# A recurrent branch on one core: four channel tiles projected with the tokens held still, and the stage put in another order

## The chip, the cores and the metric

The kernel runs on one core of a Trainium2 chip. The metric is device time in microseconds (us) of one execution; the kernel before takes 966.03 us (median of three runs, 965.65 to 968.62). A change of less than about 0.3%, 2.9 us, can't be told from none by such runs.

The engines are named as the profile names them: PE is the matrix engine (PEld its weight loads), DVE the vector engine, ACT the scalar engine, POOL the general-purpose one, SP the engine that issues nearly all transfers.

## What is computed

A two-layer decoder trunk over 256 tokens of 1024 channels, all in float32. Layer 0 is FFN, recurrent block, FFN; then keys and values are made; layer 1 is FFN, attention, FFN. The change touches the recurrent block alone:

```python
def recurrent_block(x, w_in, conv_w, conv_b, w_a, b_a, w_x, b_x, lam, w_out):
    gx = x @ w_in                                   # 1024 -> 2 * 1344
    gate, rec = gx[..., :D_RNN], gx[..., D_RNN:]
    rec = causal_depthwise_conv(rec, conv_w, conv_b)  # 4 taps along the tokens
    rec = rg_lru(rec, w_a, b_a, w_x, b_x, lam)        # block-diagonal gates, then a scan along the tokens
    return (jax.nn.gelu(gate) * rec) @ w_out
```

## The kernel before

**Tiles.** The 256 tokens are two token tiles, t = 0 and 1, of 128. The 1344 recurrent channels are eleven channel tiles: ten of 126 and one of 84. Channel tiles are worked in pairs p = 0 to 5 (the last pair is the one tile of 84), and pairs in batches of two: batch 0 is tiles 0 to 3, batch 1 tiles 4 to 7, batch 2 tiles 8 to 10.

**Split weights.** Every product is made of three matmuls, because each operand is split into an upper and a lower part: upper by upper, upper by lower, lower by upper. The normalized tokens are there as `xhi` and `xlo`. Each block of weights goes through a unit: a transfer on SP's queue into `raw` (`load_raw`, five buffers), then ACT writes the upper part `whi` (L173) and DVE subtracts to get the lower part `wlo` (L177); there are nine buffers of each. SP, ACT, DVE and POOL each work strictly in their own order; PE's order is written by hand.

**Two ways to project.** The gate half is projected by gate units (`add_gate_unit`): 128 tokens are held in PE and up to 512 columns of weights move past them (L183 to L185, form 128x512), eight blocks of 128 input channels deep, two per unit. The result lies with tokens on partitions. The recurrent half is projected by rec units (`add_rec_units`, named r0 to r5 after their pair): 126 columns of weights are held and the 256 tokens move (L190 to L192, form 128x256). The result lies with channels on partitions and tokens along the row, which the convolution and the scan need.

**After the projection.** `conv(p, ps)` scales and biases the tile with ACT (L748), then DVE adds three taps (L754). `gw0` to `gw5` are the block-diagonal gates of a pair on PE (L795), followed by tanh (L809), tanh and exp (L828) on ACT, and a chain on DVE. After each second pair a batch follows: square roots on ACT (L853) and GELU of the token tile 1 gates (L856), products and scans on DVE (L861, L862, L867), then y, the product with the gate, split by ACT (L887) and DVE (L892) for the output projection. Tanh and exp share a function table with neither the roots nor the GELU, so that ACT loads a table at each change.

**Turning.** Gate values of token tile 0 for batches 0 and 1 are brought to channels on partitions by `gate_turn`: POOL copies the 16-bit halves of the values apart into `pl` (L700), a transposing transfer on SP's queue (`swap`, L216) writes `turned`, and POOL joins the halves again (`join`, L220). The others are turned on PE (L877).

**Order of the stage.** `RG_ORDER` lists what PE does: `0g3` is gate unit 3 on token tile 0, `r2` both units of pair 2, `gw1` the gates of pair 1. The order of the entries also counts time: each slot ends in a tick, `defer(n, f)` runs f some ticks later, and a purse of ticks doles out the queued DVE work. `OUT_ORDER` then gives the output projection: token tile 0 with tiles 0 to 7, token tile 1 with tiles 0 to 5, token tile 0 with tiles 8 to 10, and the rest. The tile framework orders ACT, DVE, POOL and SP from this and puts in the waits.

Of the kernel before, what the change touches and what calls it, by code (L numbers as in the profile page):

```python
# [9 lines left out]
F32 = mybir.dt.float32  # L10
F32R = mybir.dt.float32r
BF16 = mybir.dt.bfloat16
U16 = mybir.dt.uint16
# [30 lines left out]
def trunk_kernel(ctx: ExitStack, tc: tile.TileContext, A: dict, out: bass.AP):  # L44
# [17 lines left out]
    def mmbank():  # L62
        return psum.tile([P, 512], F32, tag="mm", name=nm("mm"), bufs=4)
# [17 lines left out]
    def defer(n, fn):  # L81
        pend.append([n, fn])
# [60 lines left out]
    def main_x(t, k):  # L143
        return xhi[:, k, t * P:(t + 1) * P], xlo[:, k, t * P:(t + 1) * P]
# [22 lines left out]
    def split(rawv, parts, n, pieces=1, pin=False):  # L167
        u = Unit()
        hi = wpool.tile([P, 1024], F32R, tag="whi", name=nm("whi"), bufs=WB)
        lo = wpool.tile([P, 1024], F32R, tag="wlo", name=nm("wlo"), bufs=WB)  # L170
        m = n // pieces
        for c in range(0, n, m):
            up = nc.scalar.activation(hi[:parts, c:c + m], rawv[:, c:c + m], AF.Copy)  # L173
            if settled[0] or pin:
                tc.keep_in_program_order(up)
                settled[0] = False
            nc.vector.tensor_tensor(lo[:parts, c:c + m], rawv[:, c:c + m], hi[:parts, c:c + m].bitcast(F32), ALU.subtract)  # L177
        u.hi, u.lo = hi[:parts, :n], lo[:parts, :n]
        return u
# [38 lines left out]
    def join(dst, turned):  # L218

        nc.gpsimd.tensor_copy(dst, turned.rearrange("p (h f) -> p h f", h=2))  # L220
# [436 lines left out]
    def w_in(c0, n, k0, kn):  # L657
        return A["rg_w_in"][0, k0 * P:(k0 + kn) * P, c0:c0 + n].rearrange("(k p) n -> p k n", p=P)
# [6 lines left out]
    def add_gate_unit(g, k0, kn):  # L665
        c0, nn = GCOLS[g]

        def prep():
            return split(load_raw(w_in(c0, nn, k0, kn), P, kn * nn), P, kn * nn)

        def work(t, u):
            if k0 == 0:
                gacc[(g, t)] = mmbank()
            ps = gacc[(g, t)][:, :nn]
            for j in range(kn):
                k = k0 + j
                mm3(ps, *main_x(t, k), u.hi[:, j * nn:(j + 1) * nn], u.lo[:, j * nn:(j + 1) * nn], k == 0, k == 7)
            if k0 + kn == 8:

                if t not in toks:  # L680
                    toks[t] = pools["r"].tile([P, DRNN], F32, name=f"tok{t}")
                tok = toks[t][:, c0:c0 + nn]
                if t == 0 and g < 2:
                    nc.scalar.activation(tok, ps, AF.Gelu_apprx_tanh)
                    defer(5 - 3 * g, lambda: gate_turn(g))
                else:
                    nc.scalar.activation(tok, ps, AF.Copy)
                    plain.append(tok)
        rg[f"g{sum(n[0] == 'g' and n[1] != 'w' for n in rg)}"] = len(items)
        items.append((prep, work))  # L690
# [3 lines left out]
    def gate_turn(g):  # L694

        halves = hpool.tile([P, 512], F32, tag="t1", name=nm("pl"), bufs=2).bitcast(U16)
        hv = halves.rearrange("p (h j f) -> p h j f", h=2, j=4)
        src = toks[0][:, 4 * g * RT:4 * (g + 1) * RT].bitcast(U16)
        nc.gpsimd.memset(hv[:, :, :, RT:], 0)
        nc.gpsimd.tensor_copy(hv[:, :, :, :RT], src.rearrange("p (j f h) -> p h j f", h=2, f=RT))  # L700
# [4 lines left out]
        defer(4, lambda: join(flat, turned))  # L705

    def tiles_of(p):
        return [2 * p, 2 * p + 1] if p < 5 else [10]
# [4 lines left out]
    def add_rec_units(p):  # L713
        tl = tiles_of(p)
        n = sum(width(i) for i in tl)
        c0 = DRNN + tl[0] * RT
        ks = [(0, 4), (4, 4)] if p < 5 else [(0, 8)]
        got = []
        for (k0, kn) in ks:
            def prep(k0=k0, kn=kn):  # L720
                return split(load_raw(w_in(c0, n, k0, kn), P, kn * n), P, kn * n)

            def work(t, u, k0=k0, kn=kn):
                got.append(u)
# [12 lines left out]
                conv(p, ps)  # L737
            rg[f"r{p}{'ab'[k0 // 4]}"] = len(items)
            items.append((prep, work))

    def conv(p, ps):
        tl, w = tiles_of(p), pw(p)
        if p >= 4:
            flush(("y", (p - 4) // 2))
        xc = pools["r"].tile([RT, 2, S], F32, tag="xc", name=nm("xc"), bufs=4)
        xcs[p] = xc
        for j, i in enumerate(tl):
            nc.scalar.activation(xc[:w, j, :], ps[:w, j * S:(j + 1) * S], AF.Identity,  # L748
                                 bias=par[:w, 4 * NRT + i:4 * NRT + i + 1], scale=par[:w, 3 * NRT + i:3 * NRT + i + 1])

        def taps(j, i):
            for k in (2, 1, 0):
                s = 3 - k
                nc.vector.scalar_tensor_tensor(xc[:w, j, s:], ps[:w, j * S:(j + 1) * S - s],  # L754
                                               par[:w, k * NRT + i:k * NRT + i + 1], xc[:w, j, s:], ALU.mult, ALU.add)
# [151 lines left out]
    def parts_of(g):  # L907
        return [(0, 4, RT)] if g < 2 else [(0, 2, RT), (2, 3, BLK)]

    for g in range(2):  # L910
        for k0 in range(0, 8, 2):
            add_gate_unit(g, k0, 2)
    for p in range(4):
        add_rec_units(p)
    for k0 in (0, 3, 6):
        add_gate_unit(2, k0, min(3, 8 - k0))
    add_rec_units(4)
# [1 line left out]
    for p in range(6):  # L919
        gw_unit(p)  # L920
    n_rg = len(items)
    RG_ORDER = ("0g0 0g1 0g2 0g3 0g4 0g5 0g6 0g7 1g0 1g1 r0 1g2 r1 gw0 1g3 1g4 r2 gw1 1g5 1g6 r3 gw2 1g7 "
                "0g8 0g9 0g10 r4 gw3 r5 1g8 gw4 1g9 1g10 gw5").split()
    OUT_ORDER = [0] * 8 + [1] * 6 + [0] * 3 + [1] * 5

    gbox = {}
# [543 lines left out]
```

## Time and profile before

| | |
|---|---|
| median of three runs | 966.03 us |
| the profiled execution, its own time | 965.92 us |
| its span on the core, first to last instruction | 964.2 us |
| PE busy | 955.9 us, 99% of the span |
| DVE, ACT, POOL busy | 640.7, 527.6, 218.2 us |
| TensorE clock granted | 0.999 of full speed |

The recurrent stage lies between about 189.6 us, its first projection, and about 297 us, the end of its output projection, in the times of that span. The busy time of PE is the union of matmuls that overlap: each 128x512 matmul is shown as lasting 0.39 us, though the next starts 0.23 us after it, so the pace of PE is read from starts and not from durations.

### The profile page before, as it was taken

How to read it: one execution, taken by the hardware profiler on the slowest of the kernel's cores; microseconds unless marked ns; L12 is line 12 of the kernel's file. 1: busy time of each engine (PE TensorE's matmuls, PEld its weight loads, DVE VectorE, ACT ScalarE, POOL GpSimd, SP SyncE). 2: the span in 40 equal slices, each digit the busy share in tenths (PEclk: the TensorE clock that was granted, in tenths of full speed). 3: DMA queues.
4: the chain of work that ended last, by engine and by line, in shares of the span. 5: the costliest groups of instructions: out<-in, count | busy, mean ns of one | idle time of the engine just before them, and what ended most of it. 6: DMA issues, size and time to landing. Idle time of an engine off the chain costs nothing.

```text
span 964.2 us, 12866 instructions
## 1 busy us (share of the span) xinstructions
PE 955.9 (99%) x4575; PEld 791.3 (82%) x4575; DVE 640.7 (66%) x845; ACT 527.6 (55%) x750; POOL 218.2 (23%) x221
## 2 busy tenths in 40 slices
PE   9999999999999999999999999999999999999997
PEld 6888888898878888888898888888887788888886
DVE  6658674678997666664686566665488876666642
ACT  7546453568886555443565455444366855444431
POOL 2712330130001323230003522234022012232200
PEclk9999999999999999999999999999999999999999
DMA  8787995475346787775558979878773468777731
GB/s 286 226 258 225 256 284 197 142 228 163 119 123 219 209 236 211 205 242 196 135 182 278 253 219 258 230 216 265 226 256 97 133 199 236 207 222 233 223 109 44
DMA packets 148934, 198.79 MB, mean 206 GB/s; under 512 B 67166, under 2 KB 85958, under 8 KB 148742
## 3 DMA queue, kind: packets, MB, share of 16 engines
q1 hardware_dynamic: 146182, 191.06, 65.6%
q0 software_dynamic: 2080, 6.38, 2.1%
q8 instruction: 36, 0.59, 0.2%
q10 hardware_dynamic: 608, 0.53, 0.2%
q14 instruction: 28, 0.23, 0.1%
HBM read 182.19 MB, written 3.16 MB: 192 GB/s over the span
## 4 chain that ended last, share of the span: by engine, by line
PE 95%; DVE 2%; ACT 1%; issue 1%; POOL 0%; DMA 0%; POOLq 0%; DVEq 0%; ACTq 0%
PE mm L428 16%; PE mm L429 16%; PE mm L432 16%; PE mm L183 13%; PE mm L185 13%; PE mm L184 13%; PE gt L795 2%; PE mm L1305 1%; PE mm L190 1%; PE mm L191 1%; PE mm L192 1%; PE gt L226 1%; ACT pe L1181 1%; DVE wlo L177 0%; PE tr L127 0%
## 5 line engine op out<-in xcount | busy, mean ns | idle before, releaser
L177 DVE TENSOR_TENSOR wlo<-raw,whi 128x1024 fp32r<-128x1024 f32 (+5 forms) x329 | 418.0, 1276 | 230.7 <-ACT whi L173 228.3
L173 ACT ACTIVATE whi<-raw 128x1024 fp32r<-128x1024 f32 (+5 forms) x329 | 341.9, 1045 | 308.6 <-PE mm L432 119.2
L428 PE MATMUL mm<-whi,xhi 128*128 128x512 f32 x656 | 256.6, 391 | 0.0
L429 PE MATMUL mm<-wlo,xhi 128*128 128x512 f32 x656 | 255.5, 389 | 0.0
L432 PE MATMUL mm<-whi,xlo 128*128 128x512 f32 x656 | 202.1, 389 | 0.0
L428 PEld LDWEIGHTS mm<-whi,xhi 128*128 128x128 f32 x656 | 123.2, 188 | 25.9 <-issue 0.7
L432 PEld LDWEIGHTS mm<-whi,xlo 128*128 128x128 f32 x656 | 123.1, 188 | 25.8 <-DVE xlo L240 0.2
L429 PEld LDWEIGHTS mm<-wlo,xhi 128*128 128x128 f32 x656 | 123.2, 188 | 25.4 <-DVE wlo L177 0.3
L183 PE MATMUL mm<-whi,hhi 128*128 128x512 f32 x352 | 137.2, 390 | 0.0
L185 PE MATMUL mm<-whi,hlo 128*128 128x512 f32 x352 | 137.0, 389 | 0.0
L184 PE MATMUL mm<-wlo,hhi 128*128 128x512 f32 x352 | 136.9, 389 | 0.0
L540 POOL COPY pl<-prod 128x1024 uint16<-128x1024 uint16 (+1 forms) x48 | 69.9, 1456 | 174.4 <-DMA prod<-pl 174.4
L527 POOL COPY pl<-prod 128x1024 uint16<-128x1024 uint16 (+1 forms) x48 | 66.3, 1382 | 151.9 <-DVE prod L524 86.8
L183 PEld LDWEIGHTS mm<-whi,hhi 128*128 128x128 f32 x352 | 66.1, 188 | 13.7
L185 PEld LDWEIGHTS mm<-whi,hlo 128*128 128x128 f32 x352 | 66.1, 188 | 13.7
L184 PEld LDWEIGHTS mm<-wlo,hhi 128*128 128x128 f32 x352 | 66.1, 188 | 13.6
L198 POOL TENSOR_SCALAR nv<-ss 128x1 f32<-128x1 f32 x22 | 9.6, 437 | 268.7 <-ACT junk L205 268.7
L524 DVE SCALAR_TENSOR_TENSOR prod<-mm,rstd,sil 128x512 f32<-128x512 f32 (+1 forms) x48 | 33.8, 703 | 29.5 <-PE mm L432 25.9
L515 ACT ACTIVATE sil<-mm,rstd 128x512 f32<-128x512 f32 (+1 forms) x48 | 31.0, 649 | 32.9 <-PE mm L432 25.0
L546 DVE TENSOR_TENSOR hlo<-pl,hhi 128x512 fp32r<-128x512 f32 (+1 forms) x48 | 41.2, 858 | 3.7 <-ACT hhi L545 3.7
L183 PE MATMUL mm<-whi,xhi 128*128 128x512 f32 (+1 forms) x112 | 42.8, 382 | 0.0
L185 PE MATMUL mm<-whi,xlo 128*128 128x512 f32 (+1 forms) x112 | 42.5, 379 | 0.0
(223 smaller groups left out, 1054.6 us busy)
## 6 DMA issues: line engine op xcount, KB each, us to landing
raw<-in_ffn_w_down_dram SPq DMA_DIRECT2D x88, 512.0 KB
raw<-in_ffn_w_up_dram SPq DMA_DIRECT2D x80, 512.0 KB
raw<-in_ffn_w_gate_dram SPq DMA_DIRECT2D x78, 512.0 KB
raw<-in_rg_w_in_dram SPq DMA_DIRECT2D x10, 504.0 KB
raw<-in_rg_w_out_dram SPq DMA_DIRECT2D x10, 504.0 KB
raw<-in_ffn_w_gate_dram SPq DMA_DIRECT2D x19, 256.0 KB
raw<-in_ffn_w_up_dram SPq DMA_DIRECT2D x16, 256.0 KB
raw<-in_rg_w_in_dram SPq DMA_DIRECT2D x8, 512.0 KB
```

Of the source, the lines that this page charges most:

```text
L173: up = nc.scalar.activation(hi[:parts, c:c + m], rawv[:, c:c + m], AF.Copy)
L177: nc.vector.tensor_tensor(lo[:parts, c:c + m], rawv[:, c:c + m], hi[:parts, c:c + m].bitcast(F32), ALU.subtract)
L183: nc.tensor.matmul(ps, xh, wh, start=first, stop=False)
L184: nc.tensor.matmul(ps, xh, wl, start=False, stop=False)
L185: nc.tensor.matmul(ps, xl, wh, start=False, stop=last)
L428: nc.tensor.matmul(ps, get_x(t, k)[0], u.hi[:, c], start=k == 0, stop=False)
L429: nc.tensor.matmul(ps, get_x(t, k)[0], u.lo[:, c], start=False, stop=False)
L432: nc.tensor.matmul(ps, get_x(t, k)[1], u.hi[:, c], start=False, stop=k == nk - 1)
L524: nc.vector.scalar_tensor_tensor(pr[:, :nn], ps, rs[t][:, 0:1], s, ALU.mult, ALU.mult)
L527: nc.gpsimd.tensor_copy(halves.rearrange("p (h f) -> p h f", h=2), pr[:, :nn].bitcast(U16).rearrange("p (f h) -> p h f", h=2))
L540: nc.gpsimd.tensor_copy(halves.rearrange("p (f h) -> p h f", h=2), turned.rearrange("p (h a) b -> p h (a b)", h=2))
L546: keep(nc.vector.tensor_tensor(lv, x, hv.bitcast(F32), ALU.subtract))
```

## The change

The four channel tiles of pairs 0 and 1 are no longer projected by rec units. New units R0 to R3 (`add_tok_unit`) hold 128 tokens and move 504 columns of weights past them, as the gate units do: two blocks of input channels per unit, for both token tiles. The result `rtok` is copied from the accumulator by ACT (L725). POOL copies its halves apart into `pl` (L730), a transposing transfer turns it, and POOL writes it into its half of `rT` (L737), once for each token tile. The convolutions of pairs 0 and 1 then read `rT` in place of an accumulator, and start seven and eight ticks after the second token tile's last R unit.

The list of the stage is rewritten: R units first, the gate unit loads of group 1 behind pair 2's. `gate_turn` runs two ticks after its GELU for both groups.

```diff
-                    defer(5 - 3 * g, lambda: gate_turn(g))
+                    defer(2, lambda: gate_turn(g))
...
+    def add_tok_unit(k0, kn):
+        nn = 4 * RT
+        def prep():
+            return split(load_raw(w_in(DRNN, nn, k0, kn), P, kn * nn), P, kn * nn)
+        def work(t, u):
+            if k0 == 0:
+                racc[t] = mmbank()
+            ps = racc[t][:, :nn]
+            for j in range(kn):
+                k = k0 + j
+                mm3(ps, *main_x(t, k), u.hi[:, j * nn:(j + 1) * nn], u.lo[:, j * nn:(j + 1) * nn], k == 0, k == 7)
+            if k0 + kn == 8:
+                tok = pools["r"].tile([P, 4, P], F32, tag="y", name=nm("rtok"), bufs=2).rearrange("p a b -> p (a b)")
+                nc.scalar.activation(tok[:, :nn], ps, AF.Copy)
+                halves = pools["r"].tile([P, 2, S], F32, tag="xc", name=nm("pl"), bufs=4).rearrange("p a b -> p (a b)")
...
+                nc.gpsimd.memset(hv[:, :, :, RT:], 0)
+                nc.gpsimd.tensor_copy(hv[:, :, :, :RT],
+                                      tok[:, :nn].bitcast(U16).rearrange("p (j f h) -> p h j f", h=2, f=RT))
+                if t == 0:
+                    rtok["T"] = pools["r"].tile([P, 4, S], F32, tag="tt", name=nm("rT"), bufs=3)
+                turned = tok.bitcast(U16)
+                dst = rtok["T"][:, :, t * P:(t + 1) * P].bitcast(U16).rearrange("p a (b h) -> p h a b", h=2)
+                defer(1, lambda: swap(turned, halves))
+                defer(4, lambda: nc.gpsimd.tensor_copy(dst, turned.rearrange("p (h a b) -> p h a b", h=2, a=4)))
+                if t == 1:
+                    for p in range(2):
+                        defer(7 + p, lambda p=p: conv(p, rtok["T"][:, 2 * p:2 * p + 2, :].rearrange("p a b -> p (a b)")))
...
-    RG_ORDER = ("0g0 0g1 0g2 0g3 0g4 0g5 0g6 0g7 1g0 1g1 r0 1g2 r1 gw0 1g3 1g4 r2 gw1 1g5 1g6 r3 gw2 1g7 "
-                "0g8 0g9 0g10 r4 gw3 r5 1g8 gw4 1g9 1g10 gw5").split()
+    RG_ORDER = ("0R0 0R1 0R2 0R3 0g0 0g1 0g2 0g3 1R0 1R1 1R2 1R3 1g0 1g1 1g2 1g3 r2 0g4 0g5 0g6 0g7 gw0 1g4 gw1 "
+                "1g5 r3 gw2 1g6 1g7 0g8 0g9 0g10 r4 gw3 r5 1g8 gw4 1g9 1g10 gw5").split()
```

On POOL, at the start of the stage, the change has these rows after the statistics of the second token tile (`rtok_356` and `rtok_375` are the two token tiles of the new projection, `tok0` the gates of token tile 0):

```order
L730 COPY pl_357_1826<-rtok_356_1824 128x8x126
L699 MEMSET pl_366_1904 128x8x2
L699 MEMSET pl_408_2129 128x8x2
L737 COPY rT_358_1829<-rtok_356_1824 128x2x4x128
L700 COPY pl_366_1904<-tok0_1882 128x8x126
L220 COPY tokT_368_1908<-turned_367_1907 128x2x512
L730 COPY pl_376_1935<-rtok_375_1933 128x8x126
L737 COPY rT_358_1829<-rtok_375_1933 128x2x4x128
```

Before, only the two gate groups were turned here. Now the join of the gates' group 0 (L220) stands ahead of the copy that opens the turning of `rtok` for token tile 1 (the second L730).

On ACT, late in the stage, from the y of batch 1 to the last roots of batch 2 (`th_458`, `tt_469` belong to pairs 4 and 5, the names of 84x256 rows to pair 5), the rows before are:

```order
L887 ACTIVATE y_465_2588<-y_464_2587 126x512
L887 ACTIVATE y_465_2588<-y_467_2592 126x512
L828 ACTIVATE th_458_2533<-th_458_2533,sp4_102 126x256
L809 ACTIVATE th_470_2606<-gt_468_2597,hb_97 84x256
L809 ACTIVATE th_471_2607<-gt_468_2597,hb_97 84x256
L828 ACTIVATE tt_469_2600<-th_470_2606,sp2_101 84x256
L173 ACTIVATE whi_478_2645<-raw_477_2643 126x1024
L828 ACTIVATE th_470_2606<-th_470_2606,sp4_102 84x256
L173 ACTIVATE whi_481_2661<-raw_480_2659 126x1024
L853 ACT_TABLE_LOAD
L853 ACTIVATE tt_469_2600<-tt_469_2600 126x512
L853 ACTIVATE tt_469_2600<-tt_469_2600 84x256
```

and with the change, from the second y on:

```order
L927 ACTIVATE y_473_2561<-y_475_2565 126x512
L868 ACTIVATE tt_485_2589<-th_463_2500,sp2_101 126x256
L868 ACT_TABLE_LOAD
L868 ACTIVATE th_463_2500<-th_463_2500,sp4_102 126x256 x2
L173 ACTIVATE whi_489_2621<-raw_488_2619 126x1024
L868 ACTIVATE tt_485_2589<-th_480_2579,sp2_101 84x256
L893 ACT_TABLE_LOAD
L893 ACTIVATE tt_485_2589<-tt_485_2589 126x512
L868 ACT_TABLE_LOAD
L868 ACTIVATE th_480_2579<-th_480_2579,sp4_102 84x256
L173 ACTIVATE whi_494_2680<-raw_493_2678 126x1024
L893 ACT_TABLE_LOAD
```

The roots of pairs 4 and 5 are now apart, with the exp of pair 5 between them: two more table loads, and the exps of pair 4 stand behind the y of batch 1. The root of pair 5 follows on the last row.

On DVE, shortly before the first lower part of y for tiles 8 and 9 (`y_495` before, `y_503` with the change), the change has:

```order
L901 TENSOR_SCALAR tt_485_2589<-th_481_2580,tt_485_2589 84x256
L926 TENSOR_TENSOR y_507_2724<-tr_500_2701,tt_485_2589 126x256
L902 TENSOR_TENSOR tt_485_2589<-tt_485_2589,xc_456_2467 84x256
L177 TENSOR_TENSOR wlo_498_2694<-raw_496_2691,whi_497_2693 84x1024
L907 TENSOR_SCALAR tt_485_2589<-th_480_2579,tt_485_2589 84x256
L177 TENSOR_TENSOR wlo_506_2721<-raw_504_2718,whi_505_2720 128x1024
L926 TENSOR_TENSOR y_501_2705<-tr_499_2697,tt_485_2589 84x128
L926 TENSOR_TENSOR y_507_2724<-tr_500_2701,tt_485_2589 84x128
L932 TENSOR_TENSOR y_503_2707<-y_501_2705,y_502_2706 126x256
```

The last row, the lower part that the output projection needs for tile 8, stands behind the work of the last tile of 84 and two weight splits here as it did before; what those rows wait for is the root of pair 5. Outside the recurrent stage and the first rows of the FFN behind it the order of all engines is unchanged.

More of the change, by code (lines that the diff above doesn't have):

```diff
@@ L705, in gate_turn @@
         defer(4, lambda: join(flat, turned))
+    racc, rtok = {}, {}
+    def add_tok_unit(k0, kn):
[13 more added lines that the diff above has]
+                halves = pools["r"].tile([P, 2, S], F32, tag="xc", name=nm("pl"), bufs=4).rearrange("p a b -> p (a b)")
+                halves = halves.bitcast(U16)
+                hv = halves.rearrange("p (h j f) -> p h j f", h=2, j=4)
+                nc.gpsimd.memset(hv[:, :, :, RT:], 0)
[10 more added lines that the diff above has]
+                        defer(7 + p, lambda p=p: conv(p, rtok["T"][:, 2 * p:2 * p + 2, :].rearrange("p a b -> p (a b)")))
+        rg[f"R{k0 // 2}"] = len(items)
+        items.append((prep, work))
     def tiles_of(p):
@@ L747, in conv @@
         for j, i in enumerate(tl):
-            nc.scalar.activation(xc[:w, j, :], ps[:w, j * S:(j + 1) * S], AF.Identity,
-                                 bias=par[:w, 4 * NRT + i:4 * NRT + i + 1], scale=par[:w, 3 * NRT + i:3 * NRT + i + 1])
+            last = nc.scalar.activation(xc[:w, j, :], ps[:w, j * S:(j + 1) * S], AF.Identity,
+                                        bias=par[:w, 4 * NRT + i:4 * NRT + i + 1],
+                                        scale=par[:w, 3 * NRT + i:3 * NRT + i + 1])
+            if p < 2:
+                tc.keep_in_program_order(last)
         def taps(j, i):
@@ L908, in parts_of @@
         return [(0, 4, RT)] if g < 2 else [(0, 2, RT), (2, 3, BLK)]
[L910 to L914, printed above, removed]
+    for k0 in range(0, 8, 2):
+        add_tok_unit(k0, 2)
+    for k0 in range(0, 8, 2):
+        add_gate_unit(0, k0, 2)
+    add_rec_units(2)
+    for k0 in range(0, 8, 2):
+        add_gate_unit(1, k0, 2)
+    add_rec_units(3)
     for k0 in (0, 3, 6):
```

## The prediction

> **What bounds the kernel now.** I read the share line of the chain of waits first, then the table of waits, then the busy time of the engines over the recurrent stage, then single rows. The last chain, by engine (issue is time in which an engine waited for nothing the profile shows):
>
> ```profile
> PE 95%; DVE 2%; ACT 1%; issue 1%; POOL 0%; DMA 0%; POOLq 0%; DVEq 0%; ACTq 0%
> ```
>
> The end is set by TensorE. So the change gains what it takes off PE's queue plus what PE waits for in this stage, and loses any new wait of PE. The two waits of the stage that matter, as releaser: sum us, number, longest:
>
> ```profile
> PE gt L795 <- issue: 0.8, 1, 0.8
> ...
> DVE th L833 <- ACT th L828: 2.8, 1, 2.8
> ```
>
> The pieces of the chain with the gate matmuls (sixteen for each pair, gw0 to gw5 in the list) show where that 0.8 lies:
>
> ```profile
> 217.09 2.79 PE gt L795 x16
> ...
> 228.45 2.79 PE gt L795 x16
> ...
> 260.89 2.79 PE gt L795 x16
> ...
> 266.57 0.84 issue
> 267.41 1.06 PE gt L795 x4
> ```
>
> It is ahead of gw5. Nothing else in the stage can be gained but matmul time. The engines that feed PE are full, though; the columns are the window, its length, then busy us of PE, PEld, DVE, ACT, POOL, then clock, DMA share and GB/s:
>
> ```profile
> 231.00:245.00 14.00, 14.00 (x93) 12.18 (x90) 13.82 (x26) 13.67 (x23) 0.00 (x0) 1.00 0.57 181
> 245.00:259.00 14.00, 14.00 (x108) 13.11 (x107) 13.83 (x22) 11.64 (x20) 0.00 (x0) 1.00 0.44 162
> 268.50:291.00 22.50, 22.50 (x103) 18.36 (x103) 21.74 (x39) 18.12 (x27) 0.00 (x0) 1.00 0.44 134
> ```
>
> DVE is idle for 0.18, 0.17 and 0.76 us in these 50. ACT has 0.33, 2.36 and 4.38. PE never stops, but it is fed just in time: a longer path through ACT and DVE shows up as a wait.
>
> **The matmuls.** PE's rows, start and modelled length; pace is read from starts:
>
> ```profile
> 201.56 0.39 PE L183 MATMUL mm<-whi,xhi 128*128 128x512 f32 x1
> ...
> 204.05 0.40 PE L185 MATMUL mm<-whi,xlo 128*128 128x512 f32 x1
> 204.29 0.28 PE L190 MATMUL mm<-xhi,whi 128*126 128x256 f32 x1
> ...
> 209.79 0.28 PE L192 MATMUL mm<-xhi,wlo 128*126 128x256 f32 x1
> 209.91 0.40 PE L183 MATMUL mm<-whi,xhi 128*128 128x512 f32 x1
> ...
> 288.54 0.47 PE L185 MATMUL mm<-whi,y 126*128 126x512 f32 x1
> 288.85 0.40 PE L183 MATMUL mm<-whi,y 126*128 126x512 f32 x1
> ```
>
> From 201.56 to 204.29 are twelve 512-wide matmuls: 2.73 / 12 = 0.2275 us. From 204.29 to 209.91 are one rec unit's 48 matmuls of 256: 5.62 / 48 = 0.1171. Between them a column costs 0.1104 / 256 = 0.43 ns, so 504 columns cost 0.2275 - 8 x 0.00043 = 0.2241. The two rec units taken out held 96 x 0.1171 = 11.24 us; the eight new unit turns have 48 matmuls, 10.76 us. Term one: **-0.48 us**. If the 0.84 ahead of gw5 went too, -1.3 would be the most that can be gained.
>
> The Trainium skill ("TensorE: Matmul & The Clock Gate", section "Back-to-back issue gap") gives about 131 ns for a sustained matmul of 512 columns and 81 ns for one of 128. An estimate from that page, with 256 between them at about 98 ns, is 96 x 98 - 48 x 130 = 3.2 us gained and some 962.8 us. Our row of 0.2275 for 512 contradicts it, so it gets almost no chance.
>
> **The start of the stage.** POOL's rows first (the bracket is idle time and its releaser), then SyncE's queue, which issues the transposing transfers:
>
> ```profile
> 198.88 1.49 POOL L700 COPY pl<-tok 128x1008 uint16<-128x1008 uint16 x1 [0.16 <-ACT tok L684]
> ...
> 202.42 1.02 POOL L700 COPY pl<-tok 128x1008 uint16<-128x1008 uint16 x1 [2.00 <-ACT tok L684]
> 205.93 2.07 POOL L220 COPY tokT<-turned 128x1024 uint16<-128x1024 uint16 x1 [2.48 <-DMA turned<-pl]
> 211.16 2.36 POOL L220 COPY tokT<-turned 128x1024 uint16<-128x1024 uint16 x1 [3.16 <-DMA turned<-pl]
> ```
>
> ```profile
> 200.39 8.86 SPq L216 DMA_TRANSPOSE turned<-pl  x2
> ```
>
> A copy takes 1.02 to 1.49 us (1.25 taken), a join 2.07 to 2.36 (2.2 taken). A transfer takes between 5.5 us (200.39 to 205.93, the first, with weight loads issued just ahead of it) and 3.2 (POOL idle for 3.16 ahead of the second join). That first one also holds SyncE's queue, where the loads behind it wait.
>
> A unit has six matmuls, 1.365 us at 512 and 1.345 at 504. Ten gate units end at 204.29, so the stage runs from 204.29 - 13.65 = 190.6. With the change, sixteen token-stationary unit turns of the start, four more of gate group 1 and one rec unit stand ahead of gw0: 8 x 1.345 + 12 x 1.365 + 5.62 = 32.8, **gw0 due at 223.4** in place of 217.09. gw0 needs the convolution of pair 0, which now needs both turned halves. Three round trips share POOL and SyncE: token tile 0 of the new projection, the gates of tile 0, token tile 1; by POOL's order the second join stands ahead of the third copy.
>
> First accumulator full at 190.6 + 5.4 = 196.0; ACT's copy out ends between 196.6 and 198.7 (where POOL's first L700 got its input before), 197.5 taken. POOL's copy to 199, transfer 5.5 to 204.5, join to 206.7, gates' copy to 207.9, transfer 3.2 to 211.1, join to 213.3, copy to 214.6 (token tile 1's accumulator is full at 190.6 + 8 x 1.345 + 4 x 1.365 = 206.8), transfer to 217.8, join to 220.0. The convolution then needs one ACT pass and its taps on DVE:
>
> ```profile
> 219.21 2.42 DVE L754 SCALAR_TENSOR_TENSOR xc<-mm,par,xc 126x255 f32<-126x255 f32 x5
> ...
> 225.38 0.43 DVE L833 TENSOR_SCALAR th<-th 126x512 f32<-126x512 f32 x1 [2.76 <-ACT th L828]
> ```
>
> Five taps took 2.42, so 0.48 each; six (the two halves' three) 2.9, and the pass on ACT about 0.5: ready at 223.4, just when gw0 is due. All transfers at 3.2 give 221.1, no wait; all at 5.5 give 228.0, a wait of 4.6. I take no wait, as two of the three have no loads right ahead of them, like the 3.16 row. The memsets (0.11 each before) and the 1.02-long copies are inside the 1.25. What hides this chain is gate work already on PE's queue; without it, all of 1.25 + 3.2 + 2.2 would be bare.
>
> **The late part of the stage.** ACT's rows, and behind them the DVE rows ahead of the first lower part of y for tile 8:
>
> ```profile
> 221.84 0.61 ACT L687 ACTIVATE tok<-mm 128x512 f32<-128x512 f32 x1
> ...
> 222.96 1.28 ACT L828 ACT_TABLE_LOAD   x1
> ...
> 236.40 1.28 ACT L853 ACT_TABLE_LOAD   x1
> 237.70 1.06 ACT L853 ACTIVATE tt<-tt 126x1024 f32<-126x1024 f32 x1
> ...
> 270.65 0.60 ACT L828 ACTIVATE th<-th,sp 126x256 f32<-126x256 f32 x1
> 271.16 1.14 ACT L887 ACTIVATE y<-y 126x512 fp32r<-126x512 f32 x2
> ...
> 275.34 1.05 ACT L173 ACTIVATE whi<-raw 126x1024 fp32r<-126x1024 f32 x1
> 276.41 1.28 ACT L853 ACT_TABLE_LOAD   x1
> 277.70 0.99 ACT L853 ACTIVATE tt<-tt 126x512 f32<-126x512 f32 x2
> ```
>
> ```profile
> 282.34 0.40 DVE L861 SCALAR_TENSOR_TENSOR tt<-th,tt 84x256 f32<-84x256 f32 x1
> 282.66 1.22 DVE L177 TENSOR_TENSOR wlo<-raw,whi 126x1024 fp32r<-126x1024 f32 x1
> ...
> 286.18 0.81 DVE L886 TENSOR_TENSOR y<-tr,tt 84x128 f32<-84x128 f32 x3
> 286.91 1.21 DVE L177 TENSOR_TENSOR wlo<-raw,whi 128x1024 fp32r<-128x1024 f32 x1
> 288.04 0.62 DVE L892 TENSOR_TENSOR y<-y,y 126x256 fp32r<-126x256 f32 x2
> ```
>
> Added to ACT: two copies out (0.6 each, early, where it has gaps) and two table loads, 1.28 each and 1.30 to the next start, with the root of pair 5 last. Before, from the first y of batch 1 to the end of both roots were 278.69 - 271.16 = 7.5 us. In the new order, from that y to the root of pair 5: y twice 1.14, exps of pair 4 four at 0.5 to 0.6 (2.1), two of pair 5 (1.1), two weight splits 2.1, four table loads 5.15, roots 0.5 and 0.45: **12.5 us at the most, 12.1** with the overlap of 0.1 between neighbours that the starts show. The first y itself comes at 271.16 if gw5 waits no less than before nor more; if gw5's tanhs, which now stand ahead of it, are late by the 0.84 that gw5 waited before, at 272.0. I take 272.0, because nothing in the rows shortens that wait and two weight splits now stand ahead of y. The root of pair 5 then ends at 284.1 (283.3 at the lower end).
>
> Behind the root stands DVE's work to the lower y: before, 288.04 - 282.34 = 5.70, with three splits and four y products. Now two splits (1.13 less between starts) and three products (0.27 less): 4.3, then 0.5 until PE could use it (288.04 to 288.54), and 0.2 for hand-overs: **289.1**. PE's third matmul of tile 8 stood at 288.54 and was held for 0.08 (288.85 - 288.54 - 0.23). Without any wait it would come at 288.54 - 0.48 - 0.84 = 287.2, so this last wait swallows every earlier one of up to 1.9 us. Sum: 289.1 - 288.54 = **+0.6** (0.0 with the y at the lower end; +2.5 if DVE, with 0.76 idle in 22.5, still has two splits ahead of the root's rows). The convolutions of pairs 0 and 1 cost DVE the same taps from another memory; I put nothing for it, as five taps from an accumulator at 0.48 each bound what the cheaper memory could save to under 1 us per pair, early. The weight splits and loads keep their number and size. Behind the stage the order is the same and PE has no idle time in which to win anything back.
>
> Profiled time 965.92 + 0.6 = 966.5; the median stands 0.11 above that execution: **966.6 us**.
>
> **Rivals.** A measurement here can tell about 0.3%, 2.9 us, from no change.
>
> 1. No wait is left. DVE reaches the lower y by 287.5 since its idle time before that point was made by ACT. 965.92 - 1.3 + 0.1 = 964.7. For it: ACT has 4.38 us free in the last window. Against: 4.6 more on the way to the root is more than that. 0.14.
>
> 2. Slower: the round trips in series. One mechanism: POOL's queue takes each join ahead of the next copy, so a slow transfer delays all. It decides once token tile 1's join ends after 220.0. All at 5.5: 228.0 against 223.4, gw0 is 4.6 late, and ACT and DVE, full behind it, carry that to the end: 965.92 + 4.6 + 0.1 = 970.6. For it: the 5.54 row and the loads on the same queue. Against: the 3.16 row. 0.20.
>
> 3. Slower: gw0 and gw1 come close. gw1 is due 2.79 + 1.37 = 4.2 us behind gw0, where 228.45 - 217.09 = 11.4 lay before. DVE waited 2.76 once for ACT's tanhs, exps and table load (the row at 225.38); with two pairs on top of each other it waits a second time, and with DVE idle for 0.35 in the next 28 us that is not won back: 966.6 + 2.8 = 969.4. Against: DVE may use the second pair's convolution as cover. 0.18.
>
> 4. A drain at each table switch. If a switch cost as much again as its load, two more switches would be 5.2 in place of 2.6, so 966.6 + 2.6 = 969.2. In the rows a root starts 1.30 after its load starts (236.40 to 237.70) and the same at 276.41, so nothing of that size is there. The Trainium skill ("ScalarE: Activation LUTs", section "What ACT_TABLE_LOAD costs") puts 1283 ns for the load and 1380 ns for a drain; the first agrees with 1.28, the second does not show. 0.02.
>
> That the products do not shrink (a 504-wide moving operand at the pace of 512) is worth 0.16 us and changes none of these.
>
> **How the numbers follow.** The forecast, 966.6, has 0.37, its own range 965.5 to 968.8. With rival 1 that is 0.51 for no change, less 0.04 for the forecast's upper tail, plus 0.02 for the part of rival 3 that stays under 968.93: same 0.49. Rivals 2, 3 and 4, the tail, and 0.04 for two of them together (some 974): slower 0.20 + 0.18 + 0.02 - 0.02 + 0.04 + 0.04 = 0.46. The remainder, faster by over 2.9 us, has 0.05: the most that I can find is 1.3, so it would need something that no row shows. The range runs from 964.3, under the floor, to 972.0, over rival 2; above and below lie some 0.15.
>
> **What would show it.** Starts of 504-wide matmuls 0.224 apart. gw0 at 223.4 with no wait of PE ahead of it; a wait there, with POOL idle for a transfer ahead of a join, is rival 2. DVE waiting twice for ACT's exps between 223 and 235 is rival 3. Eleven table loads in the stage in place of nine, each 1.28. The first lower part of y for tile 8 (L932) ending near 289.1 and PE held just there. I am wrong if PE stands still anywhere between 190 and 289 for more than 2 us, or if the stage ends more than 1 us before the old one.

## The result, and the profile after

| | before | changed |
|---|---|---|
| median, us (14 runs each) | 965.66 | 969.64 |
| lowest and highest | 965.4, 968.62 | 967.59, 971.9 |
| profiled execution, time and span | 965.92, 964.2 | 969.73, 968.0 |
| ratio of times | | 1.0037, interval 1.0027 to 1.0046 |

The changed kernel is slower by 3.6 us by the ratio (2.6 to 4.4 by its interval) and by 4.0 by the medians; its runs lie further apart. The shares of the last chain, first line of that view of the changed kernel:

```profile
PE 83%; DVE 7%; ACT 3%; issue 3%; DMA 2%; POOL 2%; SPq 0%; POOLq 0%; ACTq 0%; DVEq 0%
```

PE was 95% before. From 178 us, shortly ahead of the recurrent stage, to 292 the chain now runs over DVE, ACT, POOL and a transposing transfer. Where PE waited, from its table of waits (sum us, number, longest):

```profile
PE mm L185 <- DVE y L932: 1.8, 2, 1.1
PE gt L835 <- ACT xc L785: 1.1, 1, 1.1
...
PE gt L835 <- issue: 0.6, 1, 0.6
```

PE's rows of the changed kernel, with the transposes that lead into the stage (L330) and the ones that end it (L226):

```profile
198.06 1.03 PE L330 MATMUL gt<-ident,hn 128*128 128x128 f32 x8
...
201.66 0.39 PE L183 MATMUL mm<-whi,xhi 128*128 128x504 f32 x1
...
207.16 0.39 PE L183 MATMUL mm<-whi,xhi 128*128 128x512 f32 x1
...
223.50 0.39 PE L185 MATMUL mm<-whi,xlo 128*128 128x512 f32 x1
225.04 3.03 PE L835 MATMUL gt<-xc,gw 126*126 126x256 f32 x16 [1.15 <-ACT xc L785]
...
275.16 0.39 PE L184 MATMUL mm<-wlo,y 126*128 126x512 f32 x1
276.19 0.50 PE L185 MATMUL mm<-whi,y 126*128 126x512 f32 x1 [0.64 <-DVE y L932]
...
290.40 0.39 PE L184 MATMUL mm<-wlo,y 126*128 126x512 f32 x1
291.92 0.50 PE L185 MATMUL mm<-whi,y 126*128 126x512 f32 x1 [1.12 <-DVE y L932]
...
299.88 1.04 PE L226 MATMUL gt<-ident,h 128*128 128x128 f32 x8
```

and the two rows of the kernel before that bound the same stretch:

```profile
197.95 1.03 PE L330 MATMUL gt<-ident,hn 128*128 128x128 f32 x8
...
296.47 1.04 PE L226 MATMUL gt<-ident,h 128*128 128x128 f32 x8
```

From L330 to L226 the stretch took 98.52 us before and 101.82 now: **+3.30** of the 3.8 by which the span grew. Starts before the stretch differ by 0.11, and behind it the same activation rows of the FFNs stand 3.4 later from 312 to 906 us; some 0.4 at the very end of the span is left, which nothing here explains. The last piece of DVE in the chain is 3.44 later too (960.69 before, 964.13 now), so the 0.4 lies behind the last computation. The three waits, read from starts less a matmul's 0.23, are 1.31 ahead of gw0, 0.80 at the output projection's first lower y of batch 1, and 1.29 at tile 8. This last one is the wait that the prediction let decide.

The windows shown of before, of the changed kernel (length, then busy us of PE, PEld, DVE, ACT, POOL, clock, DMA share, GB/s):

```profile
231.00:245.00 14.00, 14.00 (x92) 11.71 (x91) 13.83 (x22) 13.91 (x24) 1.33 (x1) 1.00 0.35 114
245.00:259.00 14.00, 14.00 (x105) 13.07 (x104) 13.97 (x23) 12.90 (x22) 0.00 (x0) 1.00 0.40 124
268.50:291.00 22.50, 21.58 (x96) 17.21 (x96) 20.93 (x35) 20.55 (x29) 0.00 (x0) 1.00 0.34 97
```

In these 50 us ACT is busy for 47.4 where it was 43.4. DVE, full before, is full again in the first two; in the third it is idle for 1.57 us where it was for 0.76, and PE for 0.92 where before it was never idle.

### The profile page after: what moved, and what is told of

Its sections match the earlier page's. It is cut to its first block, busy times and chain, and to the rows that moved or that the text cites. A ratio compares the mean times of both kernels' runs of the same rounds, so it can differ in the third digit from the quotient of the medians.

```text
span 968.0 us, 12783 instructions
## 1 busy us (share of the span) xinstructions
PE 955.6 (99%) x4527; PEld 788.6 (81%) x4527; DVE 653.0 (67%) x845; ACT 531.1 (55%) x754; POOL 223.2 (23%) x227
## 4 chain that ended last, share of the span: by engine, by line
PE 83%; DVE 7%; ACT 3%; issue 3%; DMA 2%; POOL 2%; SPq 0%; POOLq 0%; ACTq 0%; DVEq 0%
PE mm L428 16%; PE mm L429 16%; PE mm L432 16%; PE mm L183 11%; PE mm L185 11%; PE mm L184 11%; DVE wlo L177 2%; PE mm L1348 1%; DVE xc L794 1%; PE gt L226 1%; ACT pe L1224 1%; DVE tt L907 1%; DMA rtok<-pl 1%; DMA raw<-in_rg_w_in_dram 1%; ACT junk L205 1%
## 5 line engine op out<-in xcount | busy, mean ns | idle before, releaser
L177 DVE TENSOR_TENSOR wlo<-raw,whi 128x1024 fp32r<-128x1024 f32 (+4 forms) x329 | 427.6, 1306 | 225.4 <-ACT whi L173 224.0
L173 ACT ACTIVATE whi<-raw 128x1024 fp32r<-128x1024 f32 (+4 forms) x329 | 342.2, 1046 | 303.8 <-PE mm L432 128.6
L183 PE MATMUL mm<-whi,xhi 128*128 128x512 f32 (+2 forms) x128 | 49.1, 383 | 0.0
L185 PE MATMUL mm<-whi,xlo 128*128 128x512 f32 (+2 forms) x128 | 48.7, 381 | 0.0
L184 PE MATMUL mm<-wlo,xhi 128*128 128x512 f32 (+2 forms) x128 | 48.6, 380 | 0.0
```

The source lines that it names most:

```text
L183: nc.tensor.matmul(ps, xh, wh, start=first, stop=False)
L184: nc.tensor.matmul(ps, xh, wl, start=False, stop=False)
L185: nc.tensor.matmul(ps, xl, wh, start=False, stop=last)
```

## The experiments

The yardstick beside the time is the stretch from L330 to L226 in each one's profile, less the 98.52 of before. It leaves out what happens at the start and the end of the program. Medians of before were 965.84 to 965.89 in these groups.

| kernel | median, us | ratio to before, interval | stretch less 98.52 |
|---|---|---|---|
| changed, first profile | 969.64 | 1.0037, 1.0027 to 1.0046 | +3.30 |
| changed, second and third profile | | one time each: 968.59, 969.65 | +1.88, +1.88 |
| convolutions a tick earlier | 967.83 | 1.0018, 1.0009 to 1.0027 | +0.84 |
| gate turn after five ticks | 968.28 | 1.0024, 1.0014 to 1.0033 | +1.87 |
| roots together | 968.03 | 1.0029, 1.0017 to 1.0040 | +1.25 |
| group 1 turned by TensorE | 968.63 | 1.0034, 1.0023 to 1.0046 | +2.18 |
| before, with late gates | 966.81 | 1.0007, 0.9998 to 1.0016 | +0.93 |
| five ticks and roots | 968.09 | 1.0016, 1.0007 to 1.0025 | +1.26 |
| five ticks and convolutions | 967.48 | 1.0011, 1.0003 to 1.0020 | +0.83 |
| the same, gw0 one unit earlier | 967.13 | 1.0008, 0.9999 to 1.0016 | +0.52 |
| gates apart | 968.82 | 1.0036, 1.0022 to 1.0050 | +2.24 |
| gates early, roots together | 971.70 | 1.0060, 1.0047 to 1.0073 | +3.74 |

### The wait ahead of gw0

What held gw0, in the first profile of the changed kernel. POOL's rows, SyncE's queue and ACT:

```profile
197.50 1.81 POOL L730 COPY pl<-rtok 128x1008 uint16<-128x1008 uint16 x1 [1.13 <-ACT rtok L725]
...
204.59 2.15 POOL L737 COPY rT<-rtok 128x1024 uint16<-128x1024 uint16 x1 [5.18 <-DMA rtok<-pl]
...
218.03 1.34 POOL L737 COPY rT<-rtok 128x1024 uint16<-128x1024 uint16 x1 [3.88 <-DMA rtok<-pl]
```

```profile
214.17 1.24 SPq L216 DMA_TRANSPOSE rtok<-pl  x1
215.50 5.22 SPq L161 DMA_DIRECT2D raw<-in_rg_w_in_dram  x5
```

```profile
217.21 1.00 ACT L173 ACTIVATE whi<-raw 128x960 fp32r<-128x960 f32 x1
220.77 1.01 ACT L173 ACTIVATE whi<-raw 128x960 fp32r<-128x960 f32 x1 [2.56 <-DMA raw<-in_rg_w_in_dram]
221.68 2.07 ACT L785 ACTIVATE xc<-rT,par 126x256 f32<-126x256 f32 x4
```

Token tile 1 is turned at 218.03 + 1.34 = 219.4, but the convolution's pass on ACT (L785) starts at 221.68. Ahead of it in ACT's order stands a weight split, and the split waited 2.56 for a load that SyncE issued only at 215.50, behind the third transposing transfer. The kernel itself sets the split's place ahead of the pass: for pairs 0 and 1 it holds the convolution's passes on ACT in program order, so that they stand where the tick of the convolution puts them. Two edits try this from two sides.

```diff
-                        defer(7 + p, lambda p=p: conv(...))
+                        defer(6 + p, lambda p=p: conv(...))
```

> Edit: the convolutions of pairs 0 and 1 start one tick earlier, so on ACT the first pass of pair 0 stands ahead of a weight split that waits for its load; nothing left out. Front theory (the 1.31 us that PE waits ahead of gw0 comes from that split, and is carried to the end of the stage): gw0 waits under 0.2 us, the lower y of tile 8 ends 1 to 1.5 earlier, time about 968.3. Rival (the end of the stage is set by DVE and the roots alone): gw0 waits less, the wait at tile 8 grows by as much, time stays near 969.6. The planner also moves later rows here, so the waits decide and not the time alone.

The wait ahead of gw0 was gone (gw0 at 223.45 directly behind the unit before it), and so were those at the lower y of batch 1 and at tile 8; a wait of 0.40 in gw4 and one of 0.98 at 277.6, both on weight splits, came in their place. Runs lay between 967.16 and 968.67. The planner also put the two roots together here, so the edit is not clean.

```diff
-                    defer(2, lambda: gate_turn(g))
+                    defer(5 - 3 * g, lambda: gate_turn(g))
```

> Edit: the turn of gate group 0 starts five ticks after its GELU again, as before the change; on POOL the copy that opens token tile 1's turn then stands ahead of the join of the gates, and on SyncE's queue one load goes ahead of the gates' transfer. Nothing left out. Front theory: token tile 1's join ends 2 to 3 us earlier than 219.4, the loads behind its transfer come earlier, PE waits under 0.3 ahead of gw0, time about 968.3. Rival (the gw0 wait does not reach the end): time within 0.5 of 969.6.

This one leaves ACT's and DVE's order as it is and changes two rows on POOL and one on SyncE's queue. gw0 had no wait, and the ten runs lay within 0.5 us, 967.98 to 968.46. Token tile 1's join ended at 217.9 rather than 219.4, which is less than the 2 to 3 us that were expected. The waits behind were the same, 0.81 and 1.29, and the stretch was +1.87 in place of +3.30: without the 1.31 ahead of gw0 the end comes earlier by about as much, 1.4. One profile without that wait doesn't show that the edit took it out, as the next two runs make plain; the ten runs close together, where the changed kernel's lay between 967.59 and 971.9, speak for it.

Whether it is there in every execution was asked of the changed kernel itself, twice:

> The changed kernel once more as it is, for a second profile; its runs lie between 967.6 and 971.9. Front theory (the spread comes from when the loads land behind the transposing transfers): the wait ahead of gw0 goes with the time; at 968.5 or less it is under 0.4, at 969.5 or more it is over 1.0. Rival (the spread arises elsewhere): the wait is 1.3 again, whatever the time.

> As the run before it, a third profile of the changed kernel, with the same expectations.

At 968.59 us there was no wait ahead of gw0, as the front theory had it. Rows of PE, POOL, SyncE's queue and ACT in that execution:

```profile
223.71 0.40 PE L185 MATMUL mm<-whi,xlo 128*128 128x512 f32 x1
223.94 2.95 PE L835 MATMUL gt<-xc,gw 126*126 126x256 f32 x16
...
289.26 0.39 PE L184 MATMUL mm<-wlo,y 126*128 126x512 f32 x1
290.77 0.50 PE L185 MATMUL mm<-whi,y 126*128 126x512 f32 x1 [1.12 <-DVE y L932]
```

```profile
203.42 1.37 POOL L737 COPY rT<-rtok 128x1024 uint16<-128x1024 uint16 x1 [3.82 <-DMA rtok<-pl]
...
216.67 2.03 POOL L737 COPY rT<-rtok 128x1024 uint16<-128x1024 uint16 x1 [3.20 <-DMA rtok<-pl]
```

```profile
214.83 3.05 SPq L161 DMA_DIRECT2D raw<-in_rg_w_in_dram  x5
```

```profile
219.08 1.01 ACT L173 ACTIVATE whi<-raw 128x960 fp32r<-128x960 f32 x1 [2.79 <-DMA raw<-in_rg_w_in_dram]
```

The first transfer kept POOL idle for 3.82 here and for 5.18 in the first profile; the same weight split stood ahead of the convolution, but it started at 219.08 and gw0 was just in time. Counted from L330 (198.06 and 198.26), the split is 1.9 earlier than in the first profile. Of this 0.9 comes from the transfers: the loads behind the third one were issued that much earlier. The other 1.0 lies in the load itself: from its issue to the split were 5.27 in the first profile and 4.25 here. Why the load took longer there is open. At 969.65 the theory failed: no wait ahead of gw0 either, the stretch again +1.88, and from its first 25 us on, long before the change, the whole program 1.7 us late against the kernel before, and 1.4 against the second profile. So two things spread the runs, and the wait ahead of gw0 is only one of them. How many of the fourteen runs had it isn't known.

### The end of the stage

```diff
-                nc.scalar.activation(v, v, AF.Sqrt)
+                last = nc.scalar.activation(v, v, AF.Sqrt)
+                if g == 2:
+                    tc.keep_in_program_order(last)
```

> Edit: the roots of pairs 4 and 5 are held in program order, so they stand together behind the exps of pair 5: two table loads fewer (2.6 us of ACT), the front unchanged. Nothing left out. Root theory (the last wait of 1.29 us on the lower y of tile 8 comes from the root of pair 5 behind two more table loads): that wait falls under 0.3, time about 968.4. Rival (DVE is the one that is late there, it had work up to 287.2 against the root's end at 286.4): the wait stays above 0.8, time within 0.5 of 969.6.

Two table loads went, and the wait at tile 8 was 0.66:

```profile
288.90 0.39 PE L184 MATMUL mm<-wlo,y 126*128 126x512 f32 x1
289.79 0.50 PE L185 MATMUL mm<-whi,y 126*128 126x512 f32 x1 [0.51 <-DVE y L934]
```

That lies between the two expectations. Against the executions of the changed kernel without a wait ahead of gw0 (+1.88) the stretch is 0.63 shorter: half of the wait belongs to the roots, half does not.

```diff
-                if t == 0 and g < 2:
+                if t == 0 and g < 1:
                     nc.scalar.activation(tok, ps, AF.Gelu_apprx_tanh)
...
-            if t == 0 and g < 2:
+            if t == 0 and g < 1:
                 tps[t] = tokT[g]...
```

> Edit: gate group 1 of token tile 0 is turned by TensorE as its token tile 1 is, so POOL's copy at 225.8 and join at 231.8 and one transfer go; nothing left out. POOL theory (DVE instructions beside a POOL copy are stretched: 1.74 us beside the join where 0.68 is usual): DVE gets some 1.9 us back between 225 and 234, the waits at the first y of batch 1 and at tile 8 fall by 1 to 1.9 in sum, PE has four transposes more (0.4), time about 968.5. Rival (the stretch is covered): time 969.6 to 970.0.

The waits at the two lower y were 0.80 and 1.49, and the stretch +2.18 against +1.88. From its table of waits:

```profile
PE mm L185 <- DVE y L932: 2.0, 2, 1.3
...
PE gt L835 <- issue: 0.2, 1, 0.2
```

The 0.30 is not the four transposes that PE does more: the wait ahead of gw5, 0.6 in the changed kernel, is only 0.2 here and takes them up. Some 0.2 of it is the longer wait at tile 8. DVE did get time back (busy for 7.49 us from 225 to 234, where it was for 8.86 in the second profile), but neither wait fell. The POOL theory falls: instructions of DVE are stretched beside POOL's copies (below), but that time was not on the path.

```diff
-    RG_ORDER = ("... 1g0 1g1 r0 1g2 r1 gw0 1g3 1g4 r2 gw1 1g5 1g6 r3 gw2 1g7 ...
+    RG_ORDER = ("... 1g0 1g1 r0 1g2 r1 1g3 1g4 r2 gw0 1g5 gw1 1g6 r3 gw2 1g7 ...
```

> Edit: the kernel before, old projection and no new turn, with the gate matmuls of pairs 0 and 1 moved behind pair 2's projection in the list: gw0 at about 225.4 and gw1 4.2 behind it (before 217.1 and 228.5; with the change 223.4 and 227.8). Nothing left out. Late-gate theory (gates that come late and close together push the work of ACT and DVE of the first two pairs into the stretch where both are full, and that alone gives the waits at the first y of batch 1 and at tile 8): these two waits appear, 1 to 2 us in sum, time 967 to 968. Rival (the added work does it: two copies, two table loads, POOL's copies): time within 0.4 of the kernel before, 965.8.

The old projection with the gates late costs 0.93 in the stretch by itself, in one profile. The table of waits has a wait of 0.45 in gw4 for a weight split, but gw5's 0.84 falls to 0.23, and together they leave the first matmul of the output projection where it was. The 0.93 comes behind that: some 0.6 around 277 to 279, where PE waits for a weight split, and the rest at tile 8, where the wait is 0.26.

```profile
PE gt L795 <- ACT whi L173: 0.5, 1, 0.5
...
PE gt L795 <- issue: 0.2, 1, 0.2
```

So the late-gate theory has the direction and not its terms. The stretch lies just under the 1 to 2 that it expected, and the time, 966.81, just under 967 to 968. Of the two waits that it named only the one at tile 8 came, and smaller. The rival allowed no more than 0.4, which the stretch exceeds; the times alone don't decide, as the interval of their ratio takes in no change.

### Together, and further

> Edit: both, the turn of gate group 0 after five ticks and the two roots held together; nothing left out. Sum theory: the spread of the front goes as in the kernel with five ticks, and the wait at tile 8 is 0.66 as with the roots together: 967.6, no run above 968.2. Rival (with both, DVE's order is the bound and nothing adds up): 968.2.

The two parts added up as far as the profile goes: the stretch +1.26, the wait at tile 8 0.66. The median, 968.09, was nearer to the rival's 968.2, and some runs went to 969.5, so on the time this is inconclusive.

> Edit: the turn of gate group 0 after five ticks and the convolutions one tick earlier; the planner then also puts the two roots together and the gates' tanhs of pair 5 behind the exps of pair 4. Nothing left out. If only the work in the full stretch counts: 967.5, as the kernel with the earlier convolutions, with less spread. If the front still cost something there: 967.0 or less.

The stretch was +0.83 and the median 967.48: with the front free nothing more is gained than by the earlier convolutions alone, as the first of the two expectations had it. The smaller spread that it also named did not come (967.21 to 968.95, against 967.16 to 968.67).

```diff
-                 ... 0g4 0g5 0g6 0g7 gw0 1g4 gw1 ...
+                 ... 0g4 0g5 0g6 gw0 0g7 gw1 1g4 ...
```

> Edit: as the kernel with five ticks and earlier convolutions, and the gate matmuls of pair 0 one unit earlier in the list, before the last unit of gate group 1: due at 222.0 in place of 223.4. Nothing left out. Late-gate theory: ACT's and DVE's work of pair 0 starts 1.4 earlier, the waits behind shrink by 0.5 to 1.4, time 966.2 to 967.0. Rival (the added work does it): no gain, 967.5; if the convolution is not ready at 222.0, PE waits there and it is lost again.

gw0 came at 222.39 without a wait, the stretch was +0.52, the median 967.13: 0.35 better than the one above, less than the theory's lower end, and the best of all with the new projection. The interval of its ratio takes in no change, so by time alone this kernel can't be told from the one before. Going further needs the turned halves earlier. Two kernels moved gw0 to 219.4 and 218.0, with pair 2's projection behind it and its units loaded after group 1's. The roots stand together in both: in the first the planner left them so, in the second they are held.

```diff
-                 ... 1g2 1g3 r2 0g4 0g5 0g6 0g7 gw0 1g4 gw1 1g5 r3 ...
+                 ... 1g2 1g3 0g4 0g5 0g6 0g7 1g4 gw0 r2 gw1 1g5 r3 ...
```

> Edit: the gate units of group 1 are loaded and computed ahead of pair 2's projection, gw0 follows them and one unit more (due at 219.4), gw1 behind pair 2 (due at 227.8), five ticks for the turn of gate group 0, the convolutions two ticks earlier. Nothing left out; the planner keeps the two roots together. Late-gate theory: with the gates 8.4 apart, as they were about before (11.4), and gw0 4 us earlier, ACT works where it was idle and the stage costs no more than before: 965.5 to 966.3. Rival (the work added to ACT, DVE and POOL sets it): 967.1 to 967.5, as with the other rearranged kernels. If the turns are not done by 219.4, PE waits ahead of gw0 by what is missing.

> Edit: as the kernel with the gates apart, but gw0 directly behind the gate units of group 1 (due at 218.0) and gw1 at 226.4, the turn of gate group 0 after eight ticks so that token tile 1's turn goes first on POOL, the convolutions three ticks earlier, the roots of pairs 4 and 5 held together. Nothing left out. Late-gate theory: 965.3 to 966.0 if the convolution is ready at 218; a wait ahead of gw0 where it is not. Rival: 967.1 to 967.5.

In both PE waited ahead of or inside gw0; the row of each:

```profile
221.80 3.03 PE L835 MATMUL gt<-xc,gw 126*126 126x256 f32 x16 [2.38 <-ACT whi L173]
```

```profile
217.68 0.59 PE L835 MATMUL gt<-xc,gw 126*126 126x256 f32 x2
221.66 0.67 PE L835 MATMUL gt<-xc,gw 126*126 126x256 f32 x2 [3.38 <-issue]
```

Both got on with gw0 at 221.7 to 221.8 only, and lost what the earlier place was to bring. The first shows one thing more, in its table of waits:

```profile
PE gt L835 <- ACT whi L173: 2.4, 1, 2.4
...
PE gt L835 <- issue: 0.8, 1, 0.8
```

The second of these lies ahead of gw5, as before the change. From the starts the wait ahead of gw0 is 2.53, and the stretch less that wait is -0.29, about what the matmuls gain. With the gates apart, then, nothing was lost behind gw0; whether that holds for a PE that hasn't waited first isn't shown. In the second, token tile 1's join was done by 214.8, and still the taps of pair 0's second tile ended too late: a weight split of 2.23 us, beside POOL's copies, stood between them on DVE. Both theories' times were missed there. No version with the new projection beat the kernel before.

## Why the prediction was right and wrong

- **The number.** 969.64 lies within the range, 964.3 to 972.0, and outside the forecast's own 965.5 to 968.8. A loss of 0.6 was forecast, and 3.6 was measured; that is over the 2.9 that the prediction took for the least that can be told from no change, though the interval, 2.6 to 4.4, doesn't exclude less. Rival 3 with its 969.4 came nearest by luck, since its mechanism did not cost what it said (below).
- **What bounds the kernel.** Right. But for some 0.4 at the very end, all that was lost is wait of PE inside the stage, and none was won back behind it.
- **The matmuls: -0.48.** The sign was right, the size half. From 201.66 to 207.16 are 24 matmuls of 504 columns: 5.50 / 24 = 0.2292 apart, not 0.2241. 48 of them take 11.0 in place of 11.24, a gain of 0.24. The line through 256 and 512 columns does not hold at 504; the prediction had named that case and its price.
- **The start of the stage: no wait.** Right in two profiles, there partly by luck, and wrong in the one with 1.31. gw0's due time, 223.4, was right (PE was free at 223.73 in that profile, and gw0 began at 223.4 to 223.9 in those without a wait that don't start late). The chain of turns was costed well too: the last join ended at 219.4 against 220.0. In the second profile it ended at 218.7 - 0.3 = 218.4, and ACT's pass began 1.3 after the join: there the chain, 1.6 shorter than costed, made up for what ACT was late. What failed is the half microsecond for "the pass on ACT": it took ACT as free. The weight split ahead of that pass waits for a load, and the load for the third transfer on SyncE's queue. I had written that a transfer holds up the loads behind it, and had followed nobody who waits for those loads. That is not the rival of the round trips either, which was to cost nothing up to 220.0: the delay came by way of the loads on SyncE's queue and of ACT's order.
- **The late part: +0.6.** The mechanism was right and a size off. In the second profile, whose program starts 0.3 later, PE's third matmul of tile 8 stood at 290.77 - 0.3 = 290.5, and 290.5 - 288.54 = 1.9 is all of the stretch's +1.88: the last wait swallowed the one of 0.81 before it, as forecast. By terms: the first y came at 272.67 - 0.3 = 272.4 (272.0 taken); from it to the end of pair 5's root were 12.5 us, the sum without overlap that I had reduced to 12.1; and from there to PE 5.6, where I had 5.0, since DVE had a weight split under way when the root came. The eleven table loads came as forecast. The roots apart are only half of the last wait, though: with them together 0.66 of 1.29 stays. The prediction's "0.0 with the y at the lower end" is a slip: by its own terms it is 283.3 + 5.0 - 288.54 = -0.2. The rows:

```profile
272.67 0.64 ACT L927 ACTIVATE y<-y 126x512 fp32r<-126x512 f32 x1 [1.72 <-DVE y L926]
...
280.62 1.28 ACT L868 ACT_TABLE_LOAD   x1
...
283.49 1.28 ACT L893 ACT_TABLE_LOAD   x1
284.78 0.42 ACT L893 ACTIVATE tt<-tt 84x256 f32<-84x256 f32 x1
```

```profile
284.38 1.22 DVE L177 TENSOR_TENSOR wlo<-raw,whi 126x1024 fp32r<-126x1024 f32 x1
...
290.31 0.61 DVE L932 TENSOR_TENSOR y<-y,y 126x256 fp32r<-126x256 f32 x2
```

- **No wait left** did not come. **gw0 and gw1 close together** came in part: the old projection with such gates loses 0.93, not 2.8, and all of that behind the start of the output projection. In the first profile of the changed kernel DVE waits for the exps once, for 1.3 where it was 2.8 before; in the second and third it waits twice, as the prediction named for a sign, but for 1.7 and 1.8 in sum, less than before. **A drain at each table switch** does not show: in the rows above the root starts 1.29 after its load starts.
- **The sum as measured**, for an execution without a wait ahead of gw0: +1.88 in the stretch, of which about 0.6 goes with the roots apart and about 0.9 is what late gates cost the old kernel too. The two were tried in different kernels, so that they add up is an inference. Of the four kernels with the list of the changed one, roots together and no wait ahead of gw0, the two in which the convolutions also start a tick earlier stand at +0.84 and +0.83, near the 0.93; the two without that, at +1.25 and +1.26, are 0.4 above these. Whether the earlier convolutions bring the 0.4, or the place of pair 5's tanhs that the planner moved with them, is open. The wait ahead of gw0 adds 1.4 where it occurs. Of the time, 968.6 to 965.9 is 2.7. Of the 0.8 that the stretch does not hold, 0.3 lies ahead of it and some 0.4 behind the last rows of DVE; these stay open, and so does how often the wait occurs.

## What to carry to other kernels

When a result takes a longer way to its user (a copy, a transfer, a join), its price need not be the way itself, as the start of this stage shows: look for what stands in the same queue behind the new transfer, and who in turn waits in order behind that. Moving the users later in a list keeps PE fed at that place, but puts their elementwise work later, into a stretch where the other engines may already be full; here that cost the old projection 0.93 us in the one profile taken. Where the last of several waits on one engine decides, cost its arrival alone and without overlaps that the rows don't show.

## What the hardware showed besides

Two DVE rows of the same weight split, in the first and in the third profile of the changed kernel, with the POOL join beside them:

```profile
218.25 2.08 DVE L177 TENSOR_TENSOR wlo<-raw,whi 128x960 fp32r<-128x960 f32 x1 [0.17 <-ACT whi L173]
```

```profile
217.74 1.16 DVE L177 TENSOR_TENSOR wlo<-raw,whi 128x960 fp32r<-128x960 f32 x1 [0.17 <-ACT whi L173]
```

```profile
218.06 2.04 POOL L737 COPY rT<-rtok 128x1024 uint16<-128x1024 uint16 x1 [3.18 <-DMA rtok<-pl]
```

In the first, POOL's join began at 218.03, before DVE, and took 1.34 while DVE took 2.08. In the third DVE began first and took its usual 1.16, and the join took 2.04. In these two pairs of rows whichever starts second pays the overlap, and ends about where it would if it took its usual time only once the first has ended: 219.37 + 1.16 = 220.53 for the DVE row, which ends at 220.33, and 218.90 + 1.34 = 220.24 for the join, which ends at 220.10. The Trainium skill ("SBUF — State Buffer", section "SBUF: two separate sides") states this as an exclusive lock on a port pair that DVE and GpSimd share, held for the whole instruction; these rows agree.

The 1.7 us by which the third profile is later than the kernel before come in the main from matmuls at half pace near the start of the program, where the first profile has them 0.23 to 0.34 apart; the rows of the third:

```profile
7.75 0.63 PE L1348 MATMUL mm<-wlo,xhi 128*128 128x512 f32 x1
8.17 0.63 PE L1348 MATMUL mm<-whi,xhi 128*128 128x512 f32 x1
8.60 0.63 PE L1348 MATMUL mm<-wlo,xhi 128*128 128x512 f32 x1
9.03 0.60 PE L1348 MATMUL mm<-whi,xlo 128*128 128x512 f32 x1
```

They start 0.42 to 0.43 apart, while the granted clock of that window is given as 1.00. The Trainium skill ("TensorE: Matmul & The Clock Gate", section "Wait — 56ns, not 53.3ns?") has 426.7 ns for 512 columns on an array that is still cold, which fits. The trace bears it out: its own record of the clock begins, at full speed, at 9.5 us in this execution, where the half pace ends, and ahead of these matmuls in the others, at 3.7 in the first profile, 6.1 in the second and 5.9 in that of before. The window's 1.00 counts what lies ahead of the record as full. The record begins late, at 9.2, and the pace is halved up to there, in the profile of the kernel with five ticks and convolutions too, the longest of its eleven runs. Why it begins later in some executions is open.
